# Three early experts of a mixture-of-experts stage, from wide units of 128 rows to narrow units of 64

## The chip, the cores and the metric

The kernel runs on one core of a Trainium2 chip. The metric is the device time of one execution in microseconds; the time given for a kernel is the median of its runs. Granted clock means the share of full speed that TensorE was given.

## The reference

A transformer forward pass on 512 tokens of width 1024 in float32: two layers of a first block (hybrid attention and a gated feed-forward), then two layers of a second block, each of which ends in a mixture of experts. The change touches the mixture of experts alone:

```python
def hier_moe(h, wr_g, br_g, wr_e, br_e, w_gate, w_up, w_down):
    p_group = jax.nn.softmax((xf @ wr_g + br_g).astype(jnp.float32), axis=-1)
    p_top, g_sel = lax.top_k(p_group, 1)
    fine = (xf @ wr_e + br_e)...            # 4 groups x 8 experts
    e_val, e_sel = lax.top_k(fine, TOP_E)   # 2 experts of the chosen group
    gate = (p_top * jax.nn.softmax(e_val, axis=-1)).reshape(-1)
    ...
    # each expert, on the rows routed to it:
    (jax.nn.silu(xb @ w_gate[e]) * (xb @ w_up[e])) @ w_down[e]
    # times the gate, added into the row of its token
```

There are 32 experts, gate and up of 1024 x 512 and down of 512 x 1024, so 6.29 MB of weights each. 512 tokens with two experts each are 1024 routed rows. How many rows an expert gets is known only once the router has run. On the reference's inputs experts 0, 1 and 2 get 21, 24 and 57 rows in the first of the two expert stages, and 2, 82 and 6 in the second.

## The kernel before, in words

`moe()` (L1270) is called once per layer of the second block: stage 1 lies at about 1600 to 2080 us of the trace, stage 2 at about 2450 to 2960. Each call first normalises the tokens and runs the router, tile by tile of 128 tokens, in an order written out by hand (`ORDER`, L42); the last tile goes through `halves` (L1403) and `select` (L1370). Then it computes a table that says which rows stand in which block of 64 rows and which expert each block belongs to, and from there it works through **units**.

A unit is one set of expert weights, loaded as 12 chunks of 512 KB (4 each of gate, up and down), and the rows that use it:

- A *narrow* unit has one block of 64 rows. `products` (L1682) multiplies the turned rows with gate and up straight from the loaded float32 chunks, two halves per unit (L1695); `compute_narrow` (L1707) does the SiLU (L1711, ScalarE), the product and the down matmuls (L1722).
- A *wide* unit has two blocks, 128 rows. Its weights are first split into a high and a low part (`split`; L483 on ScalarE makes the high part, L484 on VectorE the low one), and every product is three matmuls on these parts (L488, L489, L490). `compute_wide` (L1732) has its SiLU at L1736. For unit 0 the low parts of gate and of nothing else are made on GpSimd (`split_eng`, L1678).
- A *double* unit is two wide blocks on the same split weights.

`turn` (L1660) transposes the rows of a block and then asks GpSimd to gather the rows of the block after next (`fetch`, L1626); `scatter` (L1631) adds the results into the output rows by an indirect transfer, also on GpSimd.

The chunks live in a ring of 29 buffers. The load of chunk n + 29 is issued by `load_chunk` (L1341, SyncE's queue) when chunk n has been read, that is, split or used in its last matmul. The first 28 loads are issued while the router is still at work. They can be, because the first `PRE` = 3 experts are always in the first three units, whatever the router says: for these experts the table reserves `col[:, 20]` = 2 blocks each (L92), and the first three units are wide ones. Experts with more rows than fit get further units in the order of the table, with their weights loaded again.

The order of the units is fixed in the program (L1313 to L1318): the three early ones, then a list of narrow ones into which two double and two wide units are inserted at the places of `SPREAD`. Before the change this gives 0 to 2 wide, 3 to 5 narrow, 6 double, 7 to 11 narrow, 12 double, 13 narrow, 14 wide, 15 narrow, 16 wide, then narrow units to the end. `SURE` says how many units each stage runs without asking (26 and 28); further ones are under a condition on the number of blocks, and did not run in the trace. TensorE's order is written out: the first half of the next unit's gate and up products stands before the down product of the unit at hand.

```python
units = [(b, ((b, 1),)) for b in range(b0 + 2 * BIG[1], NB)]
for b, at in zip(bigs, SPREAD):
    units.insert(at, b)
units = [(2 * s, ((2 * s, 2),)) for s in range(PRE)] + units
...
for i in n:
    load_chunk(i + RD)
```

Of the kernel before, what the change touches and what calls it, by code (L numbers as in the profile page):

```python
# [19 lines left out]
OP = mybir.AluOpType  # L20
# [5 lines left out]
D = 1024  # L26
# [3 lines left out]
NFF = 22  # L30
ALPHA = 4.0 ** 0.25
NEG = -1.0e30
NB = 60
NRING = 10
SURE = 26, 28
PRE = 3
BIG = 2, 2
SPREAD = 3, 9, 11, 13
OOB = 2048
AHEAD = 2  # L40

# [9 lines left out]
def constants():  # L51
# [8 lines left out]
    a, b = p[:, None], p[None, :]  # L60
# [18 lines left out]
    q = np.arange(64)  # L79
    e = q % 32  # L80
    pre, left = e < PRE, q >= 32
    key = np.where(pre, -100.0 + 10 * e, e / 64)
    col = np.zeros((128, 24), f)
# [4 lines left out]
    for jj in range(2):  # L88
        for t in range(NT):
            col[:, 4 + NT * jj + t] = (t * 128 + p) // 8 - OOB // 8  # L90
            col[:, 12 + NT * jj + t] = p % 8
    col[:64, 20] = np.where(pre, 2.0, 0.0)  # L92
    c["c_col"] = col
    row = np.zeros((128, 96 + NB), f)
    row[:, :64] = key + 1000.0 * left
# [5 lines left out]
    n = np.arange(0, 2048)  # L101
# [292 lines left out]
class Kern:  # L394
# [875 lines left out]
    def moe(self, l, op, nxt):  # L1270
        nc, tc, I = self.nc, self.tc, self.I
        ds, sure = bass.ds, SURE[l]
        v, sc = nc.vector, nc.scalar
        hrow = self.dram.tile([T, D], F32, name="hrow%d" % l)
        xrow = self.dram.tile([T, D], F32, name="xrow%d" % l)
        with ExitStack() as es:
            pa = es.enter_context(tc.tile_pool(name="moe", bufs=1, reuse_waits="tile"))
            gp = nc.gpsimd
# [5 lines left out]
            xg = [z[:, 3 * D:].bitcast(F32) for z in (xlf, xhf)]  # L1284

            keep = pa.tile([128, 4 * NB + 1], F32, name="keep")
            ci, gs, ei, eu = keep[:, :NB].bitcast(I32), keep[:, NB:2 * NB], keep[:1, 2 * NB:3 * NB + 1].bitcast(I32), keep[:1, 3 * NB + 1:].bitcast(I32)
# [15 lines left out]
            W = {}  # L1303
# [6 lines left out]
                return [(s, w, 2 * h + q) for q in range(2) for w in range(2)]  # L1310
            seq = half(0, 0)

            b0 = 2 * PRE + 4 * BIG[0]  # L1313
            bigs = [(b, ((b, 2), (b + 2, 2))) for b in range(2 * PRE, b0, 4)] + [(b, ((b, 2),)) for b in range(b0, b0 + 2 * BIG[1], 2)]
            units = [(b, ((b, 1),)) for b in range(b0 + 2 * BIG[1], NB)]
            for b, at in zip(bigs, SPREAD):
                units.insert(at, b)
            units = [(2 * s, ((2 * s, 2),)) for s in range(PRE)] + units  # L1318
            blocks = [b for _, u in units for b in u]
            index = {b: i for i, (b, _) in enumerate(blocks)}  # L1320
            for s in range(len(units)):
# [68 lines left out]
            hs, lows, rt = {}, {}, {}  # L1390
# [97 lines left out]
            px, pc = self.mm(), self.mm()  # L1488
# [5 lines left out]
            for u in range(1, NT):  # L1494
                nc.tensor.matmul(p4[:, u:], trib[:, 1], m34[:, :NT - u, :32], start=False, stop=(u == NT - 1), skip_group_check=True)
            col, row = c["c_col"], c["c_row"]

            cc = new([nv, 8])
            n, kc, km, rank, end, m, m2, some = (cc[:, i:i + 1] for i in range(8))
# [4 lines left out]
                                   op0=OP.is_gt, op1=OP.subtract)  # L1504
# [52 lines left out]
            B = new0([128, 8, 2, NB], BF16)  # L1557
# [6 lines left out]

            ps = self.mm()
            pc, pf = ps[:, :2 * NB].rearrange("p (a b) -> p a b", b=NB), ps[:, 3 * NB:3 * NB + 2]
            for h in range(2):
                for i in range(8):
                    nc.tensor.matmul(pf[64 * h:64 * h + 64], A[:, i], B[:, i, :, h], start=(i == 0), stop=(i == 7), skip_group_check=True)
            cf = new([128, NB])  # L1570
            v.tensor_scalar(cf[:, 0:1], pf[:, 0:1], 8.0, float(OOB), op0=OP.mult, op1=OP.add)
            v.tensor_tensor(ci[:, 0:1], pf[:, 1:2], cf[:, 0:1], op=OP.add)
            gp.indirect_dma_start(out=xg[0], out_offset=None, in_=hrow[:, :], in_offset=bass.IndirectOffsetOnAxis(ap=ci[:, 0:1], axis=0),
                                  bounds_check=T - 1, oob_is_err=False)
            for h in range(2):
                hs = slice(64 * h, 64 * h + 64)
                for i in range(8):
                    nc.tensor.matmul(pc[hs, :, 1:NB - h], A[:, i], B[:, i, :, 1 + h:], start=False, stop=(i == 7), skip_group_check=True)
                v.tensor_scalar(cf[hs, 1:NB - h], pc[hs, 0, 1:NB - h], 8.0, float(OOB), op0=OP.mult, op1=OP.add)
                v.tensor_tensor(ci[hs, 1:NB - h], pc[hs, 1, 1:NB - h], cf[hs, 1:NB - h], op=OP.add)  # L1580

# [93 lines left out]

            G = {}

            def split_eng(s, w, q):  # L1678
                if (s, w) == (0, 0):
                    return gp  # L1680

            def products(s, h):  # L1682

                parts = units[s][1]
                m = nc.tensor.matmul
                if h == 0:
                    G[s] = [[bank() for _ in range(1 if narrow(s) else 2)] for _ in parts]
                for q in (2 * h, 2 * h + 1):
                    n = [place[s, w, q] for w in range(2)]
                    if narrow(s):  # L1690
                        x, p = xT[index[parts[0][0]] % 2], G[s][0][0]
                        for k in range(2):
                            kk = 2 * q + k
                            for w in range(2):
                                m(p[64 - 64 * w:128 - 64 * w], x[:, kk], W[n[w]][:, k], start=kk == 0, stop=kk == KD - 1, skip_group_check=True)  # L1695
                    else:
                        for w in range(2):
                            hi, lo = self.split(W[n[w]], [2, 512], split_eng(s, w, q))
                            for p, (b, _) in zip(G[s], parts):
                                xgh, xgl = rows(index[b])  # L1700
                                for k in range(2):
                                    kk = 2 * q + k
                                    self.mm3(p[w], xgh[:, kk], xgl[:, kk], hi[:, k], lo[:, k], kk == 0, kk == KD - 1)
                    for i in n:
                        load_chunk(i + RD)
# [26 lines left out]
            def compute_wide(s, more):  # L1732
                parts = units[s][1]
                i0 = index[parts[0][0]]
                for j in range(len(parts)):
                    sc.activation(sg, G[s][j][0], AF.Silu)  # L1736
                    v.tensor_tensor(sg, sg, G[s][j][1], op=OP.mult)
                    free.extend(G[s][j])
                    if more and j == 0:
                        products(s + 1, 0)  # L1740
                    self.hilo(aT[j][:, 0], aT[j][:, 1], transposes(hidden(), 128))
                py = [[bank() for _ in range(2)] for _ in parts]
                for k in range(4):
                    i = place[s, 2, k]
                    h, lo = self.split(W[i][:, 0], [D], split_eng(s, 2, k))
                    load_chunk(i + RD)
                    for j in range(len(parts)):
                        for hf in range(2):
                            cs = slice(hf * 512, hf * 512 + 512)
                            self.mm3(py[j][hf], aT[j][:, 0, k], aT[j][:, 1, k], h[:, cs], lo[:, cs], k == 0, k == 3)  # L1750
                for j, (b, _) in enumerate(parts):
                    y = ys[(i0 + j) % 2]
                    for hf in range(2):
                        cs = slice(hf * 512, hf * 512 + 512)
                        v.scalar_tensor_tensor(y[:, cs], py[j][hf], gs[:, b:b + 1], g[:, cs], op0=OP.mult, op1=OP.mult)
                    free.extend(py[j])
                    scatter(i0 + j)
# [588 lines left out]
```

## Time and profile before

| | before |
|---|---|
| time, median of 3 runs | 2995.44 us (2993.11 to 2997.84) |
| profiled execution | 2993.05 us |
| its span, first to last instruction | 2991.3 us |
| mean granted clock | 0.958 |
| busy share of TensorE, VectorE, ScalarE, GpSimd | 91%, 56%, 37%, 12% |
| HBM read, written | 607.89 MB, 30.49 MB |

Shares are averages over the whole span; the expert stages take about a third of it. There, the page's slices show transfers at 300 to 400 GB/s, where the rest of the program moves 40 to 200. Rows of the timeline give the start of an instruction in us from the start of the span, its duration, engine, line, operation, and output and inputs.

### The profile page before, as it was taken

To read this page: it belongs to the slowest core of one execution; us is meant where nothing else is said; L and a number is where in the kernel's file an instruction comes from. 1 tells how busy PE (TensorE), PEld (TensorE's weight loads), DVE (VectorE), ACT (ScalarE), POOL (GpSimd) and SP (SyncE) were. 2 spreads that over 40 slices of the span, in tenths; PEclk is the share of its full clock that TensorE was granted. 3 is DMA by queue.
4 is the path that set the end of the run, shared out by engine and by line. 5 is a ranking of instruction groups with operands and counts; after the bars stand their busy time and mean duration, and the time that the engine had idled before them with its cause. 6 is when DMAs were issued, how large, how long until landed. Compare 5 with 4: busy or idle time off the path is not lost. (4 is left out here: it accounts for less than half of the span.)

```text
span 2991.3 us, 36865 instructions
## 1 busy us (share of the span) xinstructions
PE 2729.4 (91%) x13109; PEld 1930.0 (65%) x13113; DVE 1689.7 (56%) x2951; ACT 1101.1 (37%) x1736; POOL 351.5 (12%) x298
## 2 busy tenths in 40 slices
PE   8999899999998999999977999997798988999995
PEld 7666788888765888887856654642576566546431
DVE  4446877756445777757787733521595567324312
ACT  3255333333246233333543622421335545323311
POOL 0001000000000000000561211111002002121110
PEclk9999999999999999999997999999798998999998
DMA  5114456523112545531228889998422167999996
GB/s 188 57 43 146 167 172 222 183 79 137 57 57 87 197 166 172 171 111 57 79 78 300 312 319 399 357 376 307 158 93 67 40 222 271 366 329 367 388 392 268
DMA packets 248266, 594.75 MB, mean 199 GB/s; under 512 B 29971, under 2 KB 117493, under 8 KB 247800
## 3 DMA queue, kind: packets, MB, share of 16 engines
q1 hardware_dynamic: 213392, 492.55, 45.3%
q0 software_dynamic: 26832, 81.95, 8.8%
q10 hardware_dynamic: 7832, 17.63, 1.6%
q8 instruction: 109, 1.79, 0.2%
q14 instruction: 101, 0.83, 0.1%
HBM read 607.89 MB, written 30.49 MB: 213 GB/s over the span
## 5 line engine op out<-in xcount | busy, mean ns | idle before, releaser
L484 DVE TENSOR_TENSOR spt<-ringt,spt 128x1024 fp32r<-128x1024 f32 (+3 forms) x225 | 271.5, 1218 | 228.1 <-ACT spt L483 189.0
L483 ACT ACTIVATE spt<-ringt 128x1024 fp32r<-128x1024 f32 (+3 forms) x226 | 226.8, 1012 | 457.3 <-PE mm L489 237.2
L488 PE MATMUL mm<-xh,spt 128*128 128x512 f32 x848 | 342.2, 404 | 2.9 <-DVE sm L2146 1.8
L489 PE MATMUL mm<-xl,spt 128*128 128x512 f32 x848 | 335.6, 396 | 0.0
L490 PE MATMUL mm<-xh,spt 128*128 128x512 f32 x848 | 335.3, 395 | 0.1
L488 PE MATMUL acc<-spt,xh 128*128 128x512 f32 (+2 forms) x560 | 215.4, 388 | 5.9 <-ACT spt L483 5.9
L489 PE MATMUL acc<-spt,xh 128*128 128x512 f32 (+2 forms) x560 | 213.1, 381 | 0.3 <-DVE spt L484 0.3
L490 PE MATMUL acc<-spt,xl 128*128 128x512 f32 (+2 forms) x560 | 211.3, 378 | 0.0
L488 PEld LDWEIGHTS mm<-xh,spt 128*128 128x128 f32 x848 | 162.3, 191 | 44.3 <-DVE sm L816 2.8
L490 PEld LDWEIGHTS mm<-xh,spt 128*128 128x128 f32 x848 | 161.8, 191 | 35.1 <-DVE spt L484 0.6
L489 PEld LDWEIGHTS mm<-xl,spt 128*128 128x128 f32 x848 | 162.1, 191 | 34.4 <-issue 2.2
L484 DVE TENSOR_TENSOR spt<-mring,spt 128x1024 fp32r<-128x1024 f32 x104 | 132.2, 1287 | 76.6 <-ACT spt L483 69.3
L1695 PE MATMUL acc<-mring,mring 128*64 128x512 f32 x540 | 147.2, 613 | 3.6 <-DMA mring<-in_moe_w_up_dram 3.6
L483 ACT ACTIVATE spt<-mring 128x1024 fp32r<-128x1024 f32 x112 | 117.0, 1057 | 85.3 <-PE acc L490 55.3
L483 ACT ACTIVATE fsplit<-ringt 128x1024 fp32r<-128x1024 f32 x77 | 80.8, 1058 | 154.5 <-PE mm L489 52.7
L971 DVE SCALAR_TENSOR_TENSOR ada<-adaw,consts,ada 128x512 f32<-128x512 f32 x168 | 125.1, 746 | 8.4 <-DMA adaw<-in_ada_w_dram 7.0
L488 PEld LDWEIGHTS acc<-spt,xh 128*128 128x128 f32 x560 | 107.7, 193 | 33.2 <-issue 6.9
L484 DVE TENSOR_TENSOR fsplit<-ringt,fsplit 128x1024 fp32r<-128x1024 f32 x77 | 93.2, 1221 | 56.8 <-ACT fsplit L483 56.7
L488 PE MATMUL mm<-xh,fsplit 128*128 128x512 f32 x312 | 124.2, 398 | 0.0
L490 PE MATMUL mm<-xh,fsplit 128*128 128x512 f32 x312 | 123.1, 395 | 0.0
L489 PE MATMUL mm<-xl,fsplit 128*128 128x512 f32 x312 | 123.1, 394 | 0.0
L489 PEld LDWEIGHTS acc<-spt,xh 128*128 128x128 f32 x560 | 107.4, 192 | 20.2 <-DVE spt L484 1.7
(588 smaller groups left out, 5591.6 us busy)
## 6 DMA issues: line engine op xcount, KB each, us to landing
mring<-in_moe_w_gate_dram SPq DMA_DIRECT2D x160, 512.0 KB
mring<-in_moe_w_up_dram SPq DMA_DIRECT2D x160, 512.0 KB
mring<-in_moe_w_down_dram SPq DMA_DIRECT2D x145, 512.0 KB
adaw<-in_ada_w_dram POOLq DMA_DIRECT2D x48, 1024.0 KB, 6.1
ringt<-in_w_up_dram SPq DMA_DIRECT2D x44, 1024.0 KB
ringt<-in_moe_w_down_dram SPq DMA_DIRECT2D x54, 512.0 KB
ringt<-in_moe_w_gate_dram SPq DMA_DIRECT2D x49, 512.0 KB
ringt<-in_moe_w_up_dram SPq DMA_DIRECT2D x46, 512.0 KB
```

Source lines behind the costliest of these rows:

```text
L483: self.nc.scalar.activation(h, src, AF.Copy)
L484: (eng or self.nc.vector).tensor_tensor(l, src, h.bitcast(F32), op=OP.subtract)
L488: m(out, lh, rh, start=start, stop=False, **kw)
L489: m(out, lh, rl, start=False, stop=False, **kw)
L490: m(out, ll, rh, start=False, stop=stop, **kw)
L971: v.scalar_tensor_tensor(acc, raw[:, k], self.cond[:, k0 + k:k0 + k + 1], acc, op0=OP.mult, op1=OP.add)
L1695: m(p[64 - 64 * w:128 - 64 * w], x[:, kk], W[n[w]][:, k], start=kk == 0, stop=kk == KD - 1, skip_group_check=True)
```

## The change

The three early units become narrow ones, with one reserved block each; the double and wide units are moved to later places; the number of blocks in the table falls from 60 to 57, and the second stage runs 29 units without asking instead of 28. Unit 0 has no splits any more, and with them goes the function that gave some of them to GpSimd. The first gather fetches 64 rows and needs 8 matmuls in place of 16 in front of it.

The order of units is now 0 to 8 narrow, 9 double, 10 and 11 narrow, 12 wide, 13 to 15 narrow, 16 double, 17 narrow, 18 wide, then narrow units to the end, 26 units in stage 1 and 29 in stage 2.

```diff
-NB = 60
+NB = 57
-SURE = 26, 28
+SURE = 26, 29
 PRE = 3
 BIG = 2, 2
-SPREAD = 3, 9, 11, 13
+SPREAD = 6, 12, 9, 15
...
-    col[:64, 20] = np.where(pre, 2.0, 0.0)
+    col[:64, 20] = np.where(pre, 1.0, 0.0)
...
-            b0 = 2 * PRE + 4 * BIG[0]
-            bigs = [(b, ((b, 2), (b + 2, 2))) for b in range(2 * PRE, b0, 4)] + [(b, ((b, 2),)) for b in range(b0, b0 + 2 * BIG[1], 2)]
+            b0 = PRE + 4 * BIG[0]
+            bigs = [(b, ((b, 2), (b + 2, 2))) for b in range(PRE, b0, 4)] + [(b, ((b, 2),)) for b in range(b0, b0 + 2 * BIG[1], 2)]
...
-            units = [(2 * s, ((2 * s, 2),)) for s in range(PRE)] + units
+            units = [(s, ((s, 1),)) for s in range(PRE)] + units
...
-            for h in range(2):
-                for i in range(8):
-                    nc.tensor.matmul(pf[64 * h:64 * h + 64], A[:, i], B[:, i, :, h], start=(i == 0), stop=(i == 7), skip_group_check=True)
+            for i in range(8):
+                nc.tensor.matmul(pf[:64], A[:, i], B[:, i, :, 0], start=(i == 0), stop=(i == 7), skip_group_check=True)
...
-            gp.indirect_dma_start(out=xg[0], out_offset=None, in_=hrow[:, :], in_offset=bass.IndirectOffsetOnAxis(ap=ci[:, 0:1], axis=0),
+            gp.indirect_dma_start(out=xg[0][:64], out_offset=None, in_=hrow[:, :], in_offset=bass.IndirectOffsetOnAxis(ap=ci[:64, 0:1], axis=0),
...
-
-            def split_eng(s, w, q):
-                if (s, w) == (0, 0):
-                    return gp
...
-                            hi, lo = self.split(W[n[w]], [2, 512], split_eng(s, w, q))
+                            hi, lo = self.split(W[n[w]], [2, 512])
...
-                    h, lo = self.split(W[i][:, 0], [D], split_eng(s, 2, k))
+                    h, lo = self.split(W[i][:, 0], [D])
```

In the rows of the order below, line numbers after the first change are lower by one or five in the changed kernel. On VectorE the change shows first in the routing of stage 1's last token tiles. `y` is the normalised token tile, `acc` the sums in PSUM, `xl` the low part of the turned tile, and the small tiles named `mring` hold the router's logits and keys (L1375 to L1385 are `select`):

```order
 L1411 TENSOR_TENSOR x<-x,acc 128x512
 L1413 TENSOR_TENSOR y_10715<-x,mring_10725 128x512
+L1414 TENSOR_SCALAR consts<-consts 128x1
 L1438 TENSOR_TENSOR mring_10727<-acc,mring_10727 128x36
-L484 TENSOR_TENSOR spt<-mring_10719,spt 128x1024
-L1414 TENSOR_SCALAR consts<-consts 128x1
-L533 TENSOR_TENSOR xl<-mm,xh 128x4x128 x2
 L1439 TENSOR_TENSOR mring_10727<-acc,mring_10727 128x36
 L1416 RECIPROCAL consts<-consts 128x1
 L1375 TENSOR_REDUCE mring_10727<-mring_10727 128x1
 L1418 SCALAR_TENSOR_TENSOR y_10715<-y_10715,consts,mring_10725 128x512 x2
+L533 TENSOR_TENSOR xl<-mm,xh 128x4x128 x2
```

The split of an early weight chunk is gone from the queue, and the norm of the last tile (L1414 to L1418) moves ahead of an older tile's low part.

On TensorE, unit 0 of stage 1 before, from the turn of its rows on (`spt` are split weights, `xh` and `xl` the high and low parts of the rows):

```order
L1651 MATMUL mm<-c_ident,xl 128x128 x8
L1621 UNCONDITIONAL_BRANCH
L488 MATMUL acc<-spt,xh 128x512
L489 MATMUL acc<-spt,xh 128x512
L490 MATMUL acc<-spt,xl 128x512
L488 MATMUL acc<-spt,xh 128x512
L489 MATMUL acc<-spt,xh 128x512
L490 MATMUL acc<-spt,xl 128x512
```

and the same place with the change:

```order
L1650 MATMUL mm<-c_ident,xl 128x64 x8
L1620 UNCONDITIONAL_BRANCH
L1690 MATMUL acc<-mring_10719,mring_10727 64x512 x4
L1690 MATMUL acc<-mring_10720,mring_10727 64x512 x4
L1650 MATMUL mm<-c_ident,xh 128x64 x8
L1690 MATMUL acc<-mring_10721,mring_10727 64x512 x2
L1620 UNCONDITIONAL_BRANCH
L1690 MATMUL acc<-mring_10721,mring_10727 64x512 x2
```

The matmuls now read the buffers of the ring (`mring_10719` and on) themselves, with no split between the load and the product.

## Rows read from the trace of the kernel before

**Rows 1.** Timeline of ScalarE: start us, us, engine, line, operation, out<-in, [idle before]

```profile
1817.43 0.59 ACT L1711 ACTIVATE sg<-mm 64x512 f32<-64x512 f32 x1 [2.34 <-PE mm L1695]
...
1829.99 0.59 ACT L1711 ACTIVATE sg<-acc 64x512 f32<-64x512 f32 x1 [2.34 <-PE acc L1695]
```

**Rows 2.** Timeline of TensorE, one half of a narrow unit's gate and up

```profile
1826.26 3.65 PE L1695 MATMUL acc<-mring,mring 128*64 128x512 f32 x16
```

**Rows 3.** Timeline of TensorE and ScalarE, stage 1, units 0 to 3

```profile
1640.13 0.79 PE L488 MATMUL acc<-spt,xh 128*128 128x512 f32 x1
...
1653.01 0.60 ACT L1736 ACTIVATE sg<-acc 128x512 f32<-128x512 f32 x1
...
1709.74 0.59 ACT L1711 ACTIVATE sg<-acc 64x512 f32<-64x512 f32 x1 [3.02 <-PE acc L1695]
```

**Rows 4.** Timeline of ScalarE, stage 2, units 0 and 3

```profile
2502.51 0.60 ACT L1736 ACTIVATE sg<-acc 128x512 f32<-128x512 f32 x1
...
2559.28 0.59 ACT L1711 ACTIVATE sg<-acc 64x512 f32<-64x512 f32 x1 [3.02 <-PE acc L1695]
```

**Rows 5.** Timeline of ScalarE, narrow SiLUs around a double and a wide unit

```profile
1846.07 0.60 ACT L1711 ACTIVATE sg<-acc 64x512 f32<-64x512 f32 x1 [1.86 <-PE acc L1695]
...
1898.67 0.60 ACT L1711 ACTIVATE sg<-acc 64x512 f32<-64x512 f32 x1 [2.46 <-PE acc L1695]
...
1931.77 0.60 ACT L1711 ACTIVATE sg<-mm 64x512 f32<-64x512 f32 x1 [2.48 <-PE mm L1695]
```

**Rows 6.** Timeline of ScalarE, the last two units of stage 1

```profile
2060.90 0.59 ACT L1711 ACTIVATE sg<-mm 64x512 f32<-64x512 f32 x1 [3.33 <-PE mm L1695]
...
2078.01 0.59 ACT L1711 ACTIVATE sg<-acc 64x512 f32<-64x512 f32 x1 [5.22 <-PE acc L1695]
```

**Rows 7.** Windows of stage 1: busy us of each engine, granted clock, DMA share, GB/s

```profile
core 0: us, PE busy (x) PEld busy (x) DVE busy (x) ACT busy (x) POOL busy (x), PEclk, DMA share, GB/s
1647.00:1705.00 58.00, 54.12 (x245) 40.19 (x243) 46.04 (x45) 37.14 (x41) 10.84 (x6) 1.00 0.90 306
1705.00:1764.00 59.00, 55.31 (x260) 29.77 (x260) 20.97 (x25) 19.47 (x27) 12.02 (x9) 0.97 1.02 388
1764.00:1800.00 36.00, 33.52 (x150) 19.50 (x148) 9.54 (x12) 5.96 (x9) 3.98 (x3) 0.95 0.72 231
1800.00:1888.00 88.00, 81.21 (x385) 44.30 (x384) 30.59 (x35) 26.95 (x38) 13.33 (x11) 0.98 1.03 404
1888.00:1905.00 17.00, 16.66 (x79) 11.44 (x77) 11.75 (x14) 8.58 (x10) 4.47 (x3) 1.00 0.76 242
1905.00:2070.00 165.00, 154.68 (x712) 69.04 (x712) 46.50 (x55) 40.47 (x61) 27.79 (x22) 1.00 1.02 382
```

**Rows 8.** Windows of stage 2

```profile
2496.00:2555.00 59.00, 55.11 (x251) 41.10 (x250) 47.04 (x46) 37.40 (x42) 11.28 (x7) 1.00 0.89 307
2555.00:2612.00 57.00, 51.86 (x252) 27.82 (x252) 20.43 (x23) 18.47 (x26) 10.57 (x9) 1.00 1.00 383
2612.00:2645.00 33.00, 30.52 (x144) 18.73 (x144) 9.79 (x12) 7.00 (x10) 4.14 (x3) 1.00 0.76 245
2645.00:2950.00 305.00, 284.88 (x1312) 136.16 (x1308) 93.79 (x109) 81.14 (x116) 50.21 (x40) 0.99 1.02 386
```

**Rows 9.** Timeline of VectorE, the last token tile in the routing of stage 1

```profile
1599.88 0.69 DVE L1413 TENSOR_TENSOR y<-x,mring 128x512 f32<-128x512 f32 x1
...
1602.54 2.15 DVE L1413 TENSOR_TENSOR y<-x,mring 128x512 f32<-128x512 f32 x1
...
1604.72 1.21 DVE L484 TENSOR_TENSOR spt<-mring,spt 128x1024 fp32r<-128x1024 f32 x1
```

**Rows 10.** Timeline of GpSimd beside it

```profile
1601.70 2.44 POOL L484 TENSOR_TENSOR spt<-mring,spt 128x1024 fp32r<-128x1024 f32 x1 [50.55 <-ACT spt L483]
```

**Rows 11.** Timeline of SyncE's queue: two loads of weights around the start of stage 1

```profile
1632.87 0.35 SPq L1341 DMA_DIRECT2D mring<-in_moe_w_gate_dram  x1
...
1646.91 0.34 SPq L1341 DMA_DIRECT2D mring<-in_moe_w_up_dram  x1
```

More of the change, by code (lines that the diff above doesn't have):

```diff
@@ L1566, in moe @@
             pc, pf = ps[:, :2 * NB].rearrange("p (a b) -> p a b", b=NB), ps[:, 3 * NB:3 * NB + 2]
-            for h in range(2):
-                for i in range(8):
-                    nc.tensor.matmul(pf[64 * h:64 * h + 64], A[:, i], B[:, i, :, h], start=(i == 0), stop=(i == 7), skip_group_check=True)
+            for i in range(8):
+                nc.tensor.matmul(pf[:64], A[:, i], B[:, i, :, 0], start=(i == 0), stop=(i == 7), skip_group_check=True)
             cf = new([128, NB])
-            v.tensor_scalar(cf[:, 0:1], pf[:, 0:1], 8.0, float(OOB), op0=OP.mult, op1=OP.add)
-            v.tensor_tensor(ci[:, 0:1], pf[:, 1:2], cf[:, 0:1], op=OP.add)
-            gp.indirect_dma_start(out=xg[0], out_offset=None, in_=hrow[:, :], in_offset=bass.IndirectOffsetOnAxis(ap=ci[:, 0:1], axis=0),
+            v.tensor_scalar(cf[:64, 0:1], pf[:64, 0:1], 8.0, float(OOB), op0=OP.mult, op1=OP.add)
+            v.tensor_tensor(ci[:64, 0:1], pf[:64, 1:2], cf[:64, 0:1], op=OP.add)
+            gp.indirect_dma_start(out=xg[0][:64], out_offset=None, in_=hrow[:, :], in_offset=bass.IndirectOffsetOnAxis(ap=ci[:64, 0:1], axis=0),
                                   bounds_check=T - 1, oob_is_err=False)
@@ L1577, in moe @@
                 for i in range(8):
-                    nc.tensor.matmul(pc[hs, :, 1:NB - h], A[:, i], B[:, i, :, 1 + h:], start=False, stop=(i == 7), skip_group_check=True)
+                    nc.tensor.matmul(pc[hs, :, 1:NB - h], A[:, i], B[:, i, :, 1 + h:], start=(i == 0 and h == 1), stop=(i == 7), skip_group_check=True)
                 v.tensor_scalar(cf[hs, 1:NB - h], pc[hs, 0, 1:NB - h], 8.0, float(OOB), op0=OP.mult, op1=OP.add)
```

## The prediction, made before the changed kernel ran

> **What bounds the kernel now.** I read the trace in the order in which the expert stage can be short of something: the pace of its units, the transfers that feed them, and the start of the stage.
>
> *The pace.* ScalarE does one SiLU (L1711 narrow, L1736 wide) per unit, so the distance of two such rows is the step of a unit. Two narrow units with all their weights present stand 12.56 us apart [rows 1]; in that step TensorE issues two halves of gate and up at 3.65 us [rows 2] and the down product. From the SiLU of wide unit 0 to that of narrow unit 3 lie 56.73 us in stage 1 (1709.74 - 1653.01) and 56.77 in stage 2 [rows 3, 4]: three unit steps for which three narrow ones would take 37.7. Two narrow SiLUs with a double unit between them stand 52.60 us apart, with a wide one 33.10 [rows 5]; less one narrow step these cost 40.0 and 20.5. Where the weights are late a narrow step is longer: the last of stage 1 takes 17.11 [rows 6], so 12 loads arriving at their own pace take 17.11 / 12 = 1.43 us each.
>
> *The transfers.* By stretch of stage 1 [rows 7] the core moves 388, 404 and 382 GB/s wherever TensorE takes weights as fast as they come (mean by time 389), but only 306 over the three early units, 231 over the first double and 242 over the second: there the ring of 29 buffers is full, and no load can be issued before a buffer is free. Against 389 that is 58 x (1 - 306/389) = 12.4 us, 36 x (1 - 231/389) = 14.6 and 17 x (1 - 242/389) = 6.4 of transfer time not used, 33.4 us. In stage 2, against 386, the same gives 12.1 + 12.1 = 24.2 us [rows 8]. The stage thus alternates: early it is bound by TensorE with transfers idle, late by transfers with TensorE idle. A change must help both to bring its full gain.
>
> **The change, part by part: TensorE.**
> - Three wide units become narrow: 37.68 - 56.73 = -19.05 us per stage.
> - The first products: from the first wide matmul to the first SiLU lie 1653.01 - 1640.13 = 12.88 us [rows 3], paced by splits that a narrow unit does not need. A narrow unit needs two halves of 3.65 and, between them, the turn of the next block: about 1 us, an estimate from what a step of 12.56 leaves beside 7.3 for gate and up and half of that for the down product (1.6 for two sets of transposes). That is 8.3; I take 9.6, since the engine comes to it straight from a wait for the gather: -3.3 us, between 0 and -4.6.
> - Routing ahead of it: the split of unit 0's first weights goes to GpSimd, and beside it the scaling of the last token tile on VectorE (L1413) takes 2.15 us where its first half took 0.69 [rows 9, 10]; another split, 1.21 us, stands in VectorE's queue between that and the routing's own arithmetic. The order of VectorE shows both gone. 1.46 + 1.21 = 2.67 us at most, 0 at least if the router waits for something else; I take -2.4, since the chain to the first gather runs through these instructions.
> - Sum: -24.7 us in stage 1 and as much in stage 2.
> - Reserved blocks fall from two to one for each early expert. By the reference's own routing, stage 1 gives experts 0 to 2 21, 24 and 57 rows: no unit is added. Stage 2 gives 2, 82 and 6: 18 rows of expert 1 need a unit of their own, with its weights loaded once more. One narrow step, +12.56 us: stage 2 comes to -12.1. (The third constant, 28 to 29, makes that unit an unconditional one.)
> - The 60 to 57 columns of the block table, eight matmuls fewer for the first block, and gathers of 64 rows in place of 128 lie beside each other in front of the same gather; their share is under 0.3 us in what was 12.88, and I cost them at nothing. If the gather were what all wait for, half its rows would be a small gain and not a loss.
>
> **The change, part by part: transfers.**
> - The early units no longer hold the ring full: the 12.4 (12.1) us come back, and with the double units moved from places 6 and 12 to 9 and 16 they meet a ring that the narrow units have emptied. A narrow step uses 12 loads and lets 12.56 / 1.43 = 8.8 in, so it takes 3.2 from the ring; a double gives 40.0 / 1.43 - 12 = 16 back, a wide one 2.3. From 29 the ring is empty at about the ninth unit, where the double now stands: it fills to 16 and not over. So 14.6 + 6.4 us (12.1 in stage 2) come back too.
> - Lost: unit 0's splits copied weights early, so four loads could go out in the routing, the first at 1632.87 [rows 11]; narrow matmuls read the weights in place and free nothing before the first products. Four loads of 0.524 MB at 389 are 5.4 us. Against that the first release after these moves from 1646.91 to about 1640, 7 us earlier.
> - The extra unit of stage 2 is 12 x 0.524 = 6.29 MB, at 386 GB/s 16.3 us.
> - Sum: stage 1 33.4 - 5.4 + 7 = 35 us less of transfers, stage 2 24.2 + 1.6 - 16.3 = 9.5 us less.
>
> **The sum.** A stage can gain no more than the side that gains less: stage 1 24.7 (TensorE), stage 2 9.5 (transfers), together 34.2. From it I take 4 us, because the ring now runs dry near the ninth unit and again over the last narrow units, where before only the second happened at length: -30. The profiled execution took 2993.05 us, so 2963; it is 2.4 us under the median of the three runs (2995.44), so the forecast as a median is **2965 us**. With both start terms at 0 and twice the 4 us it would be 2980, with their other ends and no such loss 2959.
>
> One rule speaks against all of this. The Trainium skill ("DMA: Bandwidth & Descriptors", section "Where 436 GB/s comes from") says that for transfers between HBM and SBUF the limit of the memory side binds, some 358 GB/s for a core. By that rule the stretches at 306 would have little to give, and by its figure the sum below for rival B would come to about +25 us, an estimate. The trace does not agree: this kernel holds 404 GB/s over 88 us and 382 over 165 [rows 7].
>
> **Rivals.**
> - *A: the waits shrink as far as the transfers allow.* Both stages gain the transfer sums, 35 + 9.5 = 44.5: 2951 us. For it: steps of 17 us at the end of each stage are waits for loads that would have come earlier. Against it: TensorE's work falls by only 24.7, so the rest must come out of some 20 us of such waits in stage 1, and the ring walk still ends dry.
> - *B: slower.* If the high rates are bursts that are only possible after a pause, the transfers already run at their limit, the mean of each stage: 151.7 MB in 423 us and 165.8 in 454 [rows 7, 8], 362 GB/s. The change adds 6.29 + 8 x 0.524 = 10.5 MB to these 317.5 and gains two times 7 us of start: 328 / 362 = 906 us against 877 + 14 = 891, so +15, 3010 us. It decides below 368 GB/s. Against it: 386 over 305 us [rows 8] is no burst.
> - *C: only stage 1 gains.* If in stage 2 the extra unit, which is the last of its stage with nothing to hide under it, costs all it has, the rest being lost in waits: -24.7 + 4, 2975 us.
> - *D: no change.* Waits for loads grow by what TensorE saves, as the ring is dry from the ninth unit on: 2995 us. The 306 GB/s over the first 58 us speak against it, since the ring was kept full there.
>
> **How the numbers follow.** The forecast has 0.68: pace and rates are both measured on the same form of unit. A has 0.12, C 0.09, D 0.05, B 0.06. The range, 2946 to 2983, holds A, the forecast with its bounds, and C, with a few us beyond A and C since both rest on rounded terms; it leaves out B, D and a rest. A measurement of this kernel can tell some 0.2%, 6 us, from no change: faster 0.68 + 0.12 + 0.09 = 0.89, the same 0.05, slower 0.06.
>
> **What would show it right or wrong.** Right: narrow SiLUs 12.56 us apart from the first unit of each stage to about the eighth; 385 to 400 GB/s from the first release on, with none of the three dips; the first long step at the eighth or ninth unit; L1413 at 0.69 us on the last tile; 29 units in stage 2 with the last one paced by its loads at 16 to 17 us. Wrong: long steps before the seventh unit, or a rate that stays near 362 with the ring empty (B); dips that remain at the doubles (the ring was full for another reason); a first SiLU no earlier against the end of routing than before (both start terms 0).

## The result and the profile after

The changed kernel takes **2950.42 us** (median of 4 runs, 2948.08 to 2959.42) against 2994.28 (4 runs, 2988.30 to 2997.84) for the kernel before: a ratio of 0.9864, 95% interval 0.9846 to 0.9881, or 41 us less (36 to 46); the two medians lie 43.9 us apart. The forecast was 2965 with a range of 2946 to 2983; rival A, in which both stages gain what the transfers allow, stood at 2951. The profiled execution takes 2950.72 us (before 2993.05), its span is 2948.8, the mean granted clock 0.959 (before 0.958).

Windows of stage 1 in the changed kernel, in the columns of [rows 7]:

```profile
core 0: us, PE busy (x) PEld busy (x) DVE busy (x) ACT busy (x) POOL busy (x), PEclk, DMA share, GB/s
...
1650.00:1700.00 50.00, 47.95 (x240) 18.17 (x238) 8.67 (x12) 8.68 (x16) 9.32 (x8) 1.00 1.03 399
1700.00:1753.00 53.00, 48.91 (x234) 18.49 (x232) 10.59 (x15) 9.88 (x18) 10.22 (x9) 1.00 1.03 401
1753.00:1800.00 47.00, 42.10 (x185) 29.90 (x184) 18.72 (x19) 16.05 (x20) 2.90 (x2) 0.96 1.03 408
...
1900.00:1950.00 50.00, 46.77 (x221) 31.98 (x218) 25.96 (x30) 20.07 (x25) 8.71 (x7) 1.00 0.99 362
...
2000.00:2040.00 40.00, 37.66 (x186) 13.89 (x184) 6.50 (x9) 6.51 (x12) 7.04 (x6) 1.00 1.02 386
```

and of stage 2, against [rows 8]:

```profile
2465.00:2568.00 103.00, 96.42 (x468) 36.50 (x464) 19.25 (x27) 18.47 (x34) 19.70 (x17) 1.00 1.03 398
2568.00:2665.00 97.00, 90.38 (x416) 56.05 (x418) 43.83 (x47) 34.44 (x45) 15.19 (x11) 1.00 1.02 381
2665.00:2765.00 100.00, 91.41 (x425) 54.41 (x422) 42.06 (x47) 34.98 (x46) 16.30 (x13) 0.98 1.02 378
2765.00:2906.00 141.00, 131.46 (x596) 51.34 (x595) 25.07 (x34) 22.96 (x40) 21.40 (x19) 1.00 1.02 391
```

The dips to 306, 231, 242, 307 and 245 GB/s are gone, but for a rest: in windows of 5 us the one from 1930 to 1935, at the second double of stage 1, has 179 GB/s at a DMA share of 0.74. Otherwise the transfers run from 15 us behind the first product to the last unit, with a DMA share of about 1.0; the lowest stretch shown has 362 GB/s, and it holds that rest. The pace, by ScalarE's timeline (units 0, 1, 3, 7, 8 and the last of stage 1, the first and last of stage 2):

```profile
1647.81 0.59 ACT L1706 ACTIVATE sg<-acc 64x512 f32<-64x512 f32 x1
...
1659.19 0.59 ACT L1706 ACTIVATE sg<-acc 64x512 f32<-64x512 f32 x1 [2.35 <-PE acc L1690]
...
1684.31 0.59 ACT L1706 ACTIVATE sg<-mm 64x512 f32<-64x512 f32 x1 [2.34 <-PE mm L1690]
...
1734.56 0.59 ACT L1706 ACTIVATE sg<-acc 64x512 f32<-64x512 f32 x1 [2.34 <-PE acc L1690]
...
1753.14 0.59 ACT L1706 ACTIVATE sg<-acc 64x512 f32<-64x512 f32 x1 [3.02 <-PE acc L1690]
...
2046.91 0.59 ACT L1706 ACTIVATE sg<-acc 64x512 f32<-64x512 f32 x1 [4.54 <-PE acc L1690]
...
2461.61 0.59 ACT L1706 ACTIVATE sg<-acc 64x512 f32<-64x512 f32 x1
...
2911.51 0.59 ACT L1706 ACTIVATE sg<-acc 64x512 f32<-64x512 f32 x1 [4.30 <-PE acc L1690]
```

Three steps take 36.50 us (1684.31 - 1647.81) where [rows 3] have 56.73, and up to unit 7 every step is 11.38 or 12.56. The step to unit 8 takes 18.58, of which 3.0 are a wait for loads and the rest is the turn of the double behind it (below).

Where the 42.5 us between the two spans went, stretch by stretch (us):

| stretch | stage 1 before, after | stage 2 before, after |
|---|---|---|
| router matmuls (L1433) behind the last output product of the layer, to the issue of the first gather | 29.21, 25.19 | 28.65, 26.71 |
| gather issued to first transposes | 7.51, 4.72 | 7.31, 3.50 |
| first transposes to first SiLU | 14.74, 14.27 | 15.10, 12.85 |
| first to last SiLU | 425.00, 399.10 | 452.77, 449.90 |
| last SiLU to that point of stage 2; to the end of the span | 373.44, 371.64 | 36.02, 37.29 |

Up to the first of these points the changed kernel was 2.1 us later (1603.63 against 1601.55), a difference that is there from 1000 us on, where the two programs do the same work. In the runs below the first gather of stage 1 is issued between 1623 and 1634 us, so whole spans carry some 5 us, up or down, that have nothing to do with the edit; stretches are the safer comparison.

The units' stretch can be split again. TensorE's own work in it is the steps without a wait: 12.56 for a narrow unit, 20.5 for a wide one, and 43.0 for a double (40.0 as the prediction had it, and 3.0 more because the step ahead of a double, which holds its turn, takes 15.6 and not 12.56 even where all loads are there). That makes 409.8 us before and 389.6 after in stage 1, 435.0 and 427.3 in stage 2. What is left is waits: 15.2 and 9.5 us in stage 1, 17.8 and 22.6 in stage 2. So work fell by 20.2 and 7.7 us, and waits by 5.7 in stage 1, while they grew by 4.8 in stage 2. The split itself is less sure than these differences: in the run with half the loads left out (below) a double stood for 51.1 us between two narrow SiLUs, where the 40.0 rest on 52.60, so some 3 us of work per stage, in both kernels, may be waits.

The start of stage 1 in the changed kernel, on TensorE and then ScalarE:

```profile
1633.54 1.15 PE L1650 MATMUL mm<-c_ident,xl 64*128 64x64 f32 x8 [1.21 <-DMA xl<-hrow,keep]
1635.37 6.43 PE L1690 MATMUL acc<-mring,mring 128*64 128x512 f32 x16 [0.69 <-ACT mring L1662]
1641.73 1.09 PE L1650 MATMUL mm<-c_ident,xh 64*128 64x64 f32 x8
1642.76 7.09 PE L1690 MATMUL acc<-mring,mring 128*64 128x512 f32 x32
```

```profile
1646.52 1.28 ACT L1706 ACT_TABLE_LOAD   x1 [3.06 <-PE acc L1690]
1647.81 0.59 ACT L1706 ACTIVATE sg<-acc 64x512 f32<-64x512 f32 x1
```

The first half of unit 0 takes 6.43 us where the same 16 matmuls take 3.65 at full pace [rows 2], and ahead of the first SiLU stands a table load of 1.28 us (the kernel before has one too, at 1651.71). The windows of that time, in the same columns, show why the half is slow:

```profile
...
1635.00:1638.00 3.00, 2.63 (x8) 0.78 (x10) 0.00 (x0) 0.32 (x1) 0.91 (x1) 0.50 0.36 111
1638.00:1641.00 3.00, 3.00 (x10) 0.94 (x8) 0.00 (x0) 0.00 (x0) 0.00 (x0) 0.50 0.32 68
1641.00:1644.00 3.00, 3.00 (x18) 1.44 (x16) 0.00 (x0) 0.60 (x1) 0.90 (x1) 1.00 0.94 355
```

The granted clock is 0.50 (1.2 GHz) up to 1641 and 1.00 (2.4 GHz) from there. In front of it TensorE had worked 2.5 of 4 us (1631 to 1635), between the small matmuls of the routing and the wait for the gather. The turn between the halves takes 1.0 us, as estimated.

### The profile page after: what moved, and what is told of

It reads as the page before. It is cut to its first block, busy times and chain, and to the rows that moved or that the text cites. A ratio compares the mean times of both kernels' runs of the same rounds, so it can differ in the third digit from the quotient of the medians.

```text
span 2948.8 us, 36403 instructions
## 1 busy us (share of the span) xinstructions
PE 2701.4 (92%) x13013; PEld 1869.7 (63%) x13013; DVE 1594.7 (54%) x2872; ACT 1024.3 (35%) x1668; POOL 328.1 (11%) x292
## 5 line engine op out<-in xcount | busy, mean ns | idle before, releaser
L484 DVE TENSOR_TENSOR spt<-ringt,spt 128x1024 fp32r<-128x1024 f32 (+2 forms) x215 | 259.0, 1218 | 217.2 <-ACT spt L483 177.6
L483 ACT ACTIVATE spt<-ringt 128x1024 fp32r<-128x1024 f32 (+3 forms) x216 | 215.0, 1009 | 440.9 <-PE mm L489 239.1
L1690 PE MATMUL acc<-mring,mring 128*64 128x512 f32 x832 | 217.9, 608 | 5.9 <-DMA mring<-in_moe_w_up_dram 4.0
L488 PE MATMUL acc<-spt,xh 128*128 128x512 f32 (+2 forms) x464 | 175.8, 383 | 8.2 <-ACT spt L483 8.2
L489 PE MATMUL acc<-spt,xh 128*128 128x512 f32 (+2 forms) x464 | 175.3, 378 | 1.5 <-DVE spt L484 1.5
L490 PE MATMUL acc<-spt,xl 128*128 128x512 f32 (+2 forms) x464 | 173.7, 375 | 0.0
L1690 PEld LDWEIGHTS acc<-mring,mring 128*64 128x64 f32 x832 | 63.9, 139 | 120.7 <-issue 95.0
L971 DVE SCALAR_TENSOR_TENSOR ada<-adaw,consts,ada 128x512 f32<-128x512 f32 x168 | 124.9, 745 | 10.9 <-DMA adaw<-in_ada_w_dram 9.7
L1662 ACT ACTIVATE mring<-mm 128x512 f32<-128x512 f32 x47 | 28.1, 597 | 258.8 <-PE mm L1650 258.8
L1633 POOL DMA_INDIRECT xrow<-y,keep x59 | 85.1, 1443 | 225.0 <-DVE y L1750 100.3
L488 PEld LDWEIGHTS acc<-spt,xh 128*128 128x128 f32 x464 | 89.2, 193 | 29.8 <-ACT spt L483 10.5
```

What stands on the lines that cost most here:

```text
L483: self.nc.scalar.activation(h, src, AF.Copy)
L484: (eng or self.nc.vector).tensor_tensor(l, src, h.bitcast(F32), op=OP.subtract)
L488: m(out, lh, rh, start=start, stop=False, **kw)
L489: m(out, lh, rl, start=False, stop=False, **kw)
L490: m(out, ll, rh, start=False, stop=stop, **kw)
L971: v.scalar_tensor_tensor(acc, raw[:, k], self.cond[:, k0 + k:k0 + k + 1], acc, op0=OP.mult, op1=OP.add)
```

## The experiments

Ratios are those against the kernel before, with their 95% interval; "against the change" compares a ratio with 0.9864.

**The places put back.**

```diff
-SPREAD = 6, 12, 9, 15
+SPREAD = 3, 9, 11, 13
```

> The change with the places of the big units put back to 3, 9, 11, 13; the early units stay narrow. Theory T (in the changed kernel the transfers never pause, and a stage takes as long as its bytes): with narrow early units the ring is no longer full at the first double (unit 6 meets 29 - 6 x 3.2 = 10 loads in store), so no pause comes back and the stages take what they take with the new places, +0 to +4 us in all against the change, with the first long narrow step later than the ninth unit. Rival P (the new places are a gain of their own, since the dips of 231 and 242 GB/s were at the doubles): the dips come back, +20 to +30 us against the change.

Measured: 2956.70 us, ratio 0.9872 (0.9858 to 0.9886), 2 us over the change by the ratios and 6 by the medians. Its windows of stage 1, with the first double in the second of them, show no dip there, but one at the second double, in the last:

```profile
1650.00:1690.00 40.00, 37.95 (x192) 14.55 (x192) 6.50 (x9) 6.89 (x13) 7.10 (x6) 1.00 1.03 396
1690.00:1750.00 60.00, 53.59 (x248) 30.81 (x244) 23.85 (x27) 20.60 (x28) 8.38 (x7) 0.97 1.03 401
1750.00:1800.00 50.00, 48.08 (x233) 23.02 (x233) 9.00 (x13) 6.51 (x12) 8.71 (x7) 1.00 1.01 376
...
1860.00:1880.00 20.00, 20.00 (x92) 14.45 (x91) 12.27 (x14) 8.67 (x10) 4.46 (x3) 1.00 0.77 253
```

T holds for the first double: with narrow early units the ring is no longer full there, in either of its two places. Rival P falls as far as its 20 to 30 us go, but not altogether: 20 us at 253 GB/s are 7.0 us of transfers against 389, and first to last SiLU takes 406.7 and 450.8 us, 7.6 and 0.9 over the change. So with narrow early units the new places still bring some 8 us in stage 1, more than T's 4, and next to nothing in stage 2.

**The places alone.**

```diff
 # the kernel before
-SPREAD = 3, 9, 11, 13
+SPREAD = 6, 12, 9, 15
```

> The kernel before with the new places alone; the early units stay wide. T: the early wide units still fill the ring (12 us of pause in each stage stay), TensorE's work is as before, and only waits for loads can shrink: -8 to -18 us against the kernel before, less than half of the change. P: the dips at the doubles were what cost, so most of the change's 44 us come with the places alone, -25 to -35.

Measured: 2969.77 us, ratio 0.9924 (0.9907 to 0.9941), 23 us less than before: between the two expectations, so both had it wrong. T saw the right thing, the first dip stays and those at the doubles go:

```profile
1654.00:1705.00 51.00, 47.28 (x213) 35.26 (x212) 39.16 (x40) 31.63 (x36) 6.07 (x4) 1.00 0.92 313
1705.00:1770.00 65.00, 62.01 (x311) 23.76 (x309) 11.78 (x17) 11.25 (x21) 12.05 (x11) 1.00 1.02 390
1770.00:1820.00 50.00, 46.62 (x214) 31.96 (x215) 21.96 (x25) 17.90 (x24) 5.80 (x5) 1.00 1.03 408
...
1890.00:1945.00 55.00, 48.58 (x219) 31.62 (x215) 24.05 (x26) 20.08 (x26) 6.22 (x5) 0.97 0.99 378
```

but was too small: first to last SiLU falls by 10.9 us in each stage (414.2, 441.8). TensorE does the same work here as before, so this is all waits: 15.2 + 17.8 us of them were there, and 21.8 could be had without touching TensorE. In stage 2 the stretch is even 8 us shorter than in the change, which has the unit for the 18 rows of expert 1 there besides. The two halves of the change don't add up. The places alone give 23 us and the narrow early units with the old places 38, together not 61 but 41. The likely reason is that both draw on the same idle transfers: the windows show that either alone ends the dip at the first double.

**The big units first.**

```diff
-SPREAD = 6, 12, 9, 15
+SPREAD = 0, 2, 4, 6
```

> The change with the double and wide units straight behind the three early ones (0, 2, 4, 6). The same units, the same instructions on each engine, the same bytes. T: the ring is full again while the big units run, so transfers pause, and the narrow tail waits for every load: some 25 us more in each stage, +50 against the change in all (slower than the kernel before by a few us). Rival W (TensorE's own work sets the time, as the sum of the prediction had it for stage 1): within 10 us of the change.

Measured: 3010.78 us, ratio 1.0054 (1.0035 to 1.0074): 57 us over the change with the same instructions and the same bytes, and slower than before. In stage 1:

```profile
...
1670.00:1705.00 35.00, 31.78 (x149) 21.95 (x148) 13.86 (x14) 12.34 (x15) 2.46 (x2) 1.00 1.02 395
1705.00:1725.00 20.00, 18.31 (x79) 12.04 (x78) 10.44 (x13) 6.99 (x9) 5.30 (x4) 0.91 0.62 179
1725.00:1760.00 35.00, 31.78 (x148) 21.94 (x147) 13.53 (x15) 12.33 (x15) 2.43 (x2) 0.99 0.84 293
1760.00:1800.00 40.00, 38.10 (x169) 24.57 (x169) 22.48 (x24) 16.84 (x20) 6.76 (x5) 0.96 0.86 299
...
1920.00:2060.00 140.00, 122.85 (x506) 43.08 (x506) 17.32 (x24) 17.74 (x33) 18.57 (x16) 1.00 1.02 389
```

The dips are back at the big units (179, 293, 299), and behind them the tail pays: its last eight steps take 15.8 to 17.8 us each. First to last SiLU takes 426.1 and 484.9 us, 27 and 35 more. T holds, W falls. An order is worth here what transfer time it keeps in use.

**Without the extra unit.**

```diff
-SURE = 26, 29
+SURE = 26, 28
...
+                if l == 1 and s >= sure:
+                    return
...
-            rest(sure)
+            if l == 0:
+                rest(sure)
```

> The change with the 29th unit of stage 2 and its 12 loads left out (18 rows of the last expert in the table are not added). T: the unit costs its transfers, 12 loads at 382 to 393 GB/s, 16 us, all of it seen in the time. W: it costs a narrow step of TensorE, 12.56 us. If it were hidden: 0.

Measured: 2930.31 us, ratio 0.9781 (0.9767 to 0.9795), some 25 us under the change: more than either theory had. The stretches tell why. First to last SiLU of stage 2 falls by 11.2 us (449.9 to 438.7), and the time behind it by 9.2 (37.3 to 28.1). The second part isn't the unit, or not all of it: the edit also took away the loads for units that don't run, which SyncE otherwise steps through one by one, and the condition behind which these units stand. A run below, without such loads, has 6.2 of the 9.2; the rest is open. The first part is under the 16 that T wanted and nearer to W's 12.56, so this run doesn't decide between them; the next does. The last window of this run and that of the change above differ in their rate:

```profile
...
2765.00:2895.00 130.00, 120.61 (x542) 47.07 (x542) 24.13 (x32) 21.38 (x38) 19.84 (x17) 1.00 1.01 379
```

379 GB/s against 391, 3% of 130 us or 4 us, is about what is missing from 16, if T is right. Why the rate was lower is open.

**Expert 1 of stage 2 wide instead.** Reserved blocks per early expert are 1, 1, 1 in stage 1 and 1, 2, 1 in stage 2:

```diff
...
-SURE = 26, 29
+SURE = 26, 28
...
+FIRST = (1, 1, 1), (1, 2, 1)
...
-            units = [(s, ((s, 1),)) for s in range(PRE)] + units
+            units = [(b, ((b, FIRST[l][s]),)) for s in range(PRE) for b in (sum(FIRST[l][:s]),)] + units
```

> The change with expert 1 of stage 2 back in a wide unit (82 rows in one unit), experts 0 and 2 narrow, and no 29th unit; stage 1 as in the change. T: 12 loads fewer, 16.3 us of transfers, while TensorE's work falls by 12.56 - (20.5 - 12.56) = 4.6 only; as the transfers set the stage, first to last SiLU falls by 11 to 16 us. W: by 5.

Measured: 2944.50 us, ratio 0.9840 (0.9821 to 0.9859). First to last SiLU of stage 2 takes 437.0 us, 12.9 less: T's range, not W's 5. Beside the run before this is the clearest sign that transfers bound the stage. Both leave out the same 12 loads; one takes 12.56 us of work off TensorE, the other 4.6; the stretch falls by 11.2 and by 12.9. But 3.8 us are lost ahead of it: from the gather to the first transposes 7.27 us, as before the change. The reason is the next experiment's.

**The first gather.** Two runs. First, 128 rows again:

```diff
-            for i in range(8):
-                nc.tensor.matmul(pf[:64], A[:, i], B[:, i, :, 0], start=(i == 0), stop=(i == 7), skip_group_check=True)
+            for h in range(2):
+                for i in range(8):
+                    nc.tensor.matmul(pf[64 * h:64 * h + 64], A[:, i], B[:, i, :, h], start=(i == 0), stop=(i == 7), skip_group_check=True)
...
-            gp.indirect_dma_start(out=xg[0][:64], out_offset=None, in_=hrow[:, :], in_offset=bass.IndirectOffsetOnAxis(ap=ci[:64, 0:1], axis=0),
+            gp.indirect_dma_start(out=xg[0], out_offset=None, in_=hrow[:, :], in_offset=bass.IndirectOffsetOnAxis(ap=ci[:, 0:1], axis=0),
...
```

> The change with the first gather fetching 128 rows again (and 16 matmuls for its list in place of 8). The prediction costed this at nothing. Theory G (the turn of unit 0 waits for the gather to land, and 64 rows land sooner): from the gather's issue to the first transposes 3 to 4 us more in each stage, 6 to 7 us in all. Rival N (the landing is a fixed delay, the gain came from elsewhere): 0 to 1 us.

Measured: 2957.95 us, ratio 0.9885 (0.9867 to 0.9903), with intervals that overlap those of the change; from the gather to the transposes 5.14 and 4.59 us, 0.4 and 1.1 more than in the change. So N for the larger part: 64 rows more are worth at most about 1 us, and the other 2 to 3 come from elsewhere. (The runs here that gather 64 rows with one load near by take 4.1 to 5.1 us in stage 1 and 3.2 to 4.2 in stage 2, so even that 1 us is barely out of their spread.)

They come from the loads. The first transposes in the kernel before, waiting for the gather, and SyncE's queue around its issue at 1630.76:

```profile
1638.27 1.97 PE L1651 MATMUL mm<-c_ident,xl 128*128 128x128 f32 x8 [3.90 <-DMA xl<-hrow,keep]
...
1628.92 0.33 SPq L1341 DMA_DIRECT2D mring<-in_moe_w_gate_dram  x1
1629.30 0.43 SPq L1341 DMA_DIRECT2D mring<-in_moe_w_up_dram  x1
1629.78 0.43 SPq L1341 DMA_DIRECT2D mring<-in_moe_w_gate_dram  x1
1630.25 1.62 SPq L1341 DMA_DIRECT2D mring<-in_moe_w_up_dram  x1
```

and the changed kernel's, around 1628.82:

```profile
1627.10 0.33 SPq L1341 DMA_DIRECT2D mring<-in_moe_w_gate_dram  x1
1639.08 0.33 SPq L1341 DMA_DIRECT2D mring<-in_moe_w_up_dram  x1
```

Before, five loads of 512 KB went out between 1628.92 and 1632.87 [rows 11], so the gather shared the transfer engines with them: from 1634 to 1638, while TensorE waited for it, they moved 390 GB/s. After, one did, and from 1631 to 1635 they moved 84. The second run takes the early ones out of the kernel before:

```diff
...
+                    if (s, h) == (0, 0):
+                        late.extend(n)
+                        continue
                     for i in n:
                         load_chunk(i + RD)
+                if (s, h) == (0, 1):
+                    for i in late:
+                        load_chunk(i + RD)
```

> The kernel before with the four early loads (those of unit 0's first half) issued behind the loads of its second half, so that they no longer stand in the routing. Theory C (these loads, issued 2 us after the first gather, held it up; the change lost them and so got its gather sooner): from the gather's issue to the first transposes 7.3 to 7.5 us become 4.5 to 5.5 in both stages. The whole time moves little, -5 to +5 us, since the loads are missing later. Rival N (the gather of 128 rows takes that long by itself): 7 us or more, as before.

Measured: 2992.95 us, ratio 0.9993 (0.9982 to 1.0005), no change in all. In stage 1 the gather took 4.58 us in place of 7.51, as C has it. In stage 2 it took 8.35, which looks like N until the queue is read: there the edit did not keep the loads away (buffers of unit 0's second half were apparently free by then as well):

```profile
2478.48 0.33 SPq L1341 DMA_DIRECT2D mring<-in_moe_w_gate_dram  x1
2479.44 0.33 SPq L1341 DMA_DIRECT2D mring<-in_moe_w_up_dram  x1
2479.81 0.43 SPq L1341 DMA_DIRECT2D mring<-in_moe_w_gate_dram  x1
2480.29 0.43 SPq L1341 DMA_DIRECT2D mring<-in_moe_w_up_dram  x1
```

with the gather issued at 2480.54. With four or five loads at the gather it took 7.3 to 9.3 us (both stages of the kernel before and of the places alone, this stage 2, and stage 2 with expert 1 wide, where four loads go out from 2447.96 on and a gather of 64 rows at 2449.60); with three, in stage 2 of the kernel before with half its loads, 5.5; with one or two 3.2 to 5.1. C holds as far as it speaks of the loads; its number for stage 2 was missed, because the edit did not do there what it was meant to.

**Half the loads left out in stage 2.** The same edit in the change and in the kernel before; units then compute on what the buffers hold.

```diff
-                nc.sync.dma_start(dst, src[:, ch * kk:ch * kk + kk], **kw)
+                if l == 0 or n < RD or n % 2:
+                    nc.sync.dma_start(dst, src[:, ch * kk:ch * kk + kk], **kw)
```

> The change with every second load behind the 29th left out in stage 2 alone; the units compute on what the buffer holds. Stage 1 is as it was. T: all waits of stage 2 are waits for loads, so its first to last SiLU falls from 449.9 us to TensorE's own work: 27 steps of 12.56 less 1.2 for the first, with 2 x 40.0 + 2 x 20.5 for the big units in place of four of them: some 421 us, 28.6 less. Rival W (these waits are TensorE's or VectorE's): 440 to 450.

> The kernel before with every second load behind the 29th left out in stage 2 alone. T: its waits for loads go too, 452.8 us to 56.7 + 20 x 12.56 + 2 x 40.0 + 2 x 20.5 = 429, 24 less; the difference to the same edit of the change is then TensorE's work alone, about 8 us, where the kernels as they are differ by 2.9. W: 445 to 453.

Measured: first to last SiLU of stage 2 435.9 us in the change and 440.4 before, 14.0 and 12.4 less. Both land between the expectations. More than half of the waits go with the loads, but 9 and 5 us stay over the work counted above. In the change two of them, 3.2 and 5.7 us, stand at a down product (L1718 in this kernel) behind ScalarE, which had been waiting for loads of a coming big unit: the splits of that unit (at 2673.50 and 2678.20, the second after 3.65 us of waiting for its load) stand in its order ahead of the narrow unit's own copy (2679.28). With this edit the difference between the kernels is 4.5 us, where T had 8.

**The end of a stage.** Loads of the output rows on ScalarE's queue:

```diff
-                nc.sync.dma_start(self.x[:, t], xrow[t * 128:(t + 1) * 128])
+                sc.dma_start(self.x[:, t], xrow[t * 128:(t + 1) * 128])
```

> The change with the four loads of the output rows behind each expert stage issued by ScalarE's queue instead of SyncE's. In the profile of the change they stand behind the skipped conditional loads of SyncE's queue, which end some 6 us after the last scatter was issued in stage 1. If that queue holds them: 4 to 6 us less for each stage, 8 to 12 in all. If they wait for the scatter to land: 0 to 4 in all.

Measured: 2964.32 us, ratio 0.9904 (0.9886 to 0.9923), 12 us over the change, 5 of which stand ahead of the first gather, where the edit does nothing. The loads of the rows go out 19.5 us behind the last SiLU of stage 1, in the change 18.7. A miss: ScalarE itself waits there for SyncE, 11.14 us in front of this row in stage 1:

```profile
2071.32 1.28 ACT L1784 ACT_TABLE_LOAD   x1 [11.14 <-SPq L1776]
```

So the skipped loads must go, not the queue behind them:

```diff
...
+                if s >= sure and not now:
+                    return
...
-                    e, kw = ds(regs[s, blk[0]], 1), {"cond": nb[0] > s}
+                    e, kw = ds(regs[s, blk[0]], 1), {} if now else {"cond": nb[0] > s}
...
                 with tc.If(nb[0] > units[s][0]):
+                    for n in sorted(place[s, w, ch] for w in range(3) for ch in range(4)):
+                        load_chunk(n, True)
                     compute(s)
```

> The change, with the loads of units that may not run moved into the condition under which the unit runs, so that SyncE no longer steps through 29 skipped loads at the end of each stage. Theory S (in the run without the 29th unit its 12 loads and the skipped ones were both gone, and the time from the last SiLU to the end fell by 9.2 us: that was the skipped loads): 7 to 10 us less behind the last SiLU of each stage, 14 to 20 in all. Rival L (the end of a stage waits for the last scatter to land): 0 to 5 in all.

Measured: 2943.54 us, ratio 0.9827 (0.9806 to 0.9848), 11 us under the change. The end of SyncE's queue in the change, with the last scatter issued at 2921.69:

```profile
2922.09 1.48 SPq L1341 DMA_DIRECT2D mring<-in_moe_w_down_dram  x4
2924.77 0.07 SPq L1341 DMA_DIRECT2D x<-in_moe_w_gate_dram  x1
...
2926.61 0.07 SPq L1341 DMA_DIRECT2D mring<-in_moe_w_gate_dram  x1
2930.60 1.89 SPq L1800 DMA_DIRECT2D x<-xrow  x4
```

and here, with the last scatter at 2920.48:

```profile
2904.99 0.33 SPq L1343 DMA_DIRECT2D mring<-in_moe_w_down_dram  x1
2926.91 1.84 SPq L1804 DMA_DIRECT2D x<-xrow  x4
```

A skipped load still takes SyncE 0.46 us. Without them 31.1 us lie behind the last SiLU (37.3 in the change), 6.2 less, and 5.4 less lie between the stages: some 12 in all, between S and L. Of the 6.2, 2.5 lie between the issue of the last scatter and the loads of the rows (8.9 us in the change, 6.4 here); how the others come about no run here takes apart. What is left in that place is the landing of the scatter, for which SyncE waits here.

**Both.**

> Both edits, no skipped loads and expert 1 of stage 2 wide. S and T add up, since one lies behind the last unit and the other in front of it: 25 to 34 us under the change, some 2920 us. If they don't add: about the better of the two.

Measured: 2934.77 us (2929.12 to 2940.09), ratio 0.9809 (0.9789 to 0.9829): 57 us under the kernel before (51 to 63), 16 under the change, the fastest full version here. They bring less than hoped, as each was overestimated: by their own ratios they bring 11 and 7, and these do add up within the intervals. Under other inputs the units behind `SURE` would start without loads ahead of them, which no run here shows.

## Why the prediction was right in kind and short in size

- **Which way and through what: right.** The early units hold the ring full, transfers idle there, narrow units give both TensorE and the transfers time back. Of the signs named beforehand, the spacing of 12.56 us up to the eighth unit, a first long step at the ninth, the end of the three dips, L1413 at 0.69 us on the last tile and a last unit paced by its loads in stage 2 (15.5 us, where 16 to 17 were named) are all there. The rate named, 385 to 400 GB/s, is there only in part: the stretches shown have 362 to 408.
- **The early units, -19.05 us: right.** Three steps fell by 20.2.
- **Routing, -2.4 per stage: right in sum.** -4.0 and -1.9.
- **The first gather, costed at nothing: wrong**, -2.8 and -3.8. The reason given (its share of 12.88 us is small) looked at the matmuls and rows and not at what else is on the transfer engines when the gather is issued. The same four loads that the prediction booked as lost transfer time were in the gather's way; and it took 1632.87 in [rows 11] for the first of them, where it is the last.
- **The first products, -3.3 per stage: too much**, -0.5 and -2.3. The step that failed is the estimate of 9.6 us. It took half a unit at 3.65 where TensorE came from a wait with a low granted clock (6.43; 5.01 in stage 2), and left out the table load of 1.28 us in front of the first SiLU. The prediction's 8.3 with these two comes to 12.4 and 10.9 us; 12.4 and 11.0 were measured.
- **"A stage can gain no more than the side that gains less": the step that failed.** It cost most. In stage 1 it capped the gain at TensorE's 24.7 us, and 4 were then taken off for the ring running dry. But the 15 us of waits in stage 1 before (4.6 of them in the step of [rows 6]) were themselves due to transfer time not used, and so were part of what transfers could give back: work fell by 20.2 and waits fell too, by 5.7, so that stage 1 gained 33 us, not 21 to 25 (of the 8.5 above the cap, 5.7 are these waits and most of the rest is the gather). The places alone show it: 10.9 us in each stage with TensorE's work unchanged. Rival A argued this, and its terms (35 us in stage 1, 9.5 in stage 2) are nearly what was seen; the forecast gave it 0.12.
- **Stage 2, 9.5 us: right in size, in part by luck.** It gained 10.9 up to the last SiLU, but 8.0 of these lie ahead of the first SiLU, 3.8 of them in the gather that was costed at nothing; the units' own stretch gave 2.9. The extra unit, 16.3 by its transfers and 12.56 by TensorE, cost 11.2 where it was left out.
- **The upper bound of 2980** that the prediction gives beside its sum comes to 2978 by its own terms (19.05 for stage 1 and 6.5 for stage 2, less 8); nothing hangs on it.
- **Rival B** (362 GB/s as a limit) falls: the changed kernel holds 378 to 398 GB/s over 441 us of stage 2. The rule of the Trainium skill ("DMA: Bandwidth & Descriptors", section "Where 436 GB/s comes from") by which some 358 GB/s bind does not agree with that; what other cores of the chip moved at the time, no run here shows. **C** and **D** fall with the result.

What stays open: why the rate differs between 351 and 408 GB/s in stretches where the DMA share is about 1.0, and 9 us of stage 2's steps that half the loads did not explain in the change.

## What to carry to other kernels

Where a ring alternates between full and empty, add up work and waits separately, and ask of each wait whether its cause is earlier idle transfer time: such waits are part of the gain and not a floor under it. Two remedies for the same idle time (here, cheaper early units and a better order) must not be added. And before a gather on the critical path, look at which bulk loads are issued within a few microseconds of it.

## What was not expected

- A gather of 64 or 128 rows took 3.2 to 5.1 us to the first use with one or two loads of 512 KB issued near it, 7.3 to 9.3 us with four or five.
- A load skipped by its condition still takes SyncE 0.46 us; without them 5.4 and 6.2 us less lay behind the last SiLU of the two expert stages.
- The narrow form met a granted clock of 0.50 for its first 6 us in stage 1 (6.43 us for a half of 3.65); in the kernel before, the wide unit's matmuls were back at 0.40 us each 2.3 us after the first.
